# Copies and stores of the last pair of row tiles in a three-way projection

## The chip, the cores and the metric

The kernel runs on one core of a Trainium2 chip. The metric is the device time of one execution in microseconds. A profiled execution gives a span, from the first to the last instruction of the program, and a trace of every engine; the time of that execution is a little longer than its span, because something lies around the program.

The engines in the text: TensorE (PE) multiplies matrices into accumulator banks; VectorE (DVE) and ScalarE (ACT) copy and add; GpSimd (POOL) prepares sums of the input; SyncE (SP) issues most of the transfers; ACT issues some. The transfers themselves run on 16 DMA engines that SP's and ACT's queues share.

## What is computed

```python
def reference(x, w_qkv):           # x: 16 x 512 x 768, w_qkv: 768 x 2304, float32
    qkv = np.matmul(x, w_qkv)
    hidden = x.shape[-1]
    q = qkv[..., :hidden]
    k = qkv[..., hidden:2*hidden]
    v = qkv[..., 2*hidden:]
    return np.stack([q, k, v], axis=0).astype(np.float32)
```

So 8192 rows of 768 numbers are multiplied with one matrix of 768 x 2304, and the 2304 result columns go to three outputs of 768 columns each.

## The kernel before

**Tiles.** Rows are taken in 32 pairs p of two tiles of 128 rows (`NP` = 32). Of the 2304 columns, 2048 are done as two "quads" q of 1024 columns, and 256 columns in between (`REM`) as a plain product, the remainder. A quad of a pair is a block matrix of 2 x 2 blocks, each 128 rows by 512 columns (`CB`): c11, c12 for the first row tile, c21, c22 for the second. It is made with seven block products instead of eight (a Strassen-like scheme): weight sums `ts` are made once, input sums `s` for every pair, and products 1 to 7 of a quad are added up in two accumulator banks x and y and in the output tile.

**Who does what in a quad.** `product(u, n, ps, start)` (line 258 is its matmul) is three matmuls of 128x512. `do(u, n)` issues product n and what takes its result out of the banks:

- n = 1 and 2: product 1 into x, copied to c11 by ACT (L267), product 2 into a third bank, added to c11 by DVE (L280).
- n = 6: on top of x; ACT copies x to c12 (L286).
- n = 5: into y; nothing is taken out.
- n = 7: on top of x; ACT copies x to c22 (L292), then DVE adds y to c22 (L293).
- n = 4: on top of x; ACT copies x to c21 (L296).
- n = 3: on top of y; DVE adds y to c12 (L299).

**Where blocks lie in the outputs.** The first quad has columns 0 to 1023, the second 1280 to 2303, and an output ends every 768 columns. So c12 and c22 of the first quad and c11 and c21 of the second lie across two outputs, 256 columns in each; the other blocks lie in one. Each block is 256 KB.

**Order.** The order on every engine is written out by hand. The pairs before the last go through `two` and `plain`/`summed`; the last `plain` call has `stored` set, and its two quads c and d are stored block by block with `store_cols` on SP's queue. Then `last(a, b)` does pair 31, whose quads are a (q = 0) and b (q = 1): product 1 of both; the remainder of the first row tile; product 2 of both, each with a store of c11; product 6 of both; products 5 and 7 of a with a store of c22, then those of b; products 4 and 3 of a with stores of c21 and c12, then those of b; the remainder of the second row tile. `store_cols(u, r, lo, hi, *engs)` (L404 is its transfer) cuts a block at the border of an output and issues a transfer per piece, each on the next queue of `engs`; all are on SP but for c21 of a, on ACT, and the first half of c21 of b, also on ACT. `rem_stored` multiplies the remainder into one bank (L316), has ACT copy its 256 columns (L414), and issues the store on ACT's queue (L416).

**Semaphores of the transfers.** The recording layer gives the transfers of SP and ACT eight semaphores in turn. A transfer first waits until the one that used its semaphore before has landed, and SP at the end of the program (L690) waits for all eight. Waits between engines are put in by the same layer from the tiles and banks that instructions read and write.

Of the kernel before, what the change touches and what calls it, by code (L numbers as in the profile page):

```python
# [10 lines left out]
def kernel(  # L11
# [20 lines left out]
    nc = tc.nc  # L32
    P = 128
    G = 32
    B, T, H = x.shape
    M = B * T
# [5 lines left out]
    NP = M // (2 * P)  # L42
    CB = 512
    REM = N3 - 4 * CB
    Q_OFF = (0, 2 * CB + REM)
# [4 lines left out]
    ident = mybir.ActivationFunctionType.Identity  # L50
    add = mybir.AluOpType.add
# [3 lines left out]
    out_flat = out.rearrange("s b t h -> s (b t) h")  # L55
# [184 lines left out]
    def quad(p, q, pool=o_pool, tag="o"):  # L240
        u = Quad()
        u.p, u.q = p, q
        u.o = pool.tile([P, 2, 2 * CB], fp32, name="o", tag=tag)
        u.x = u.y = u.z = None
        return u

    def product(u, n, ps, start):
        t1, t2, t3, t4 = ts[u.q]
        if n <= 2:
            h = (n - 1) * KH  # L250
            lhs = [xb[u.p][:, h + j, :P] for j in range(KH)]
            rhs = [b1[u.q][:, h + j, :] for j in range(KH)]
        else:
            k, t = {3: (4, b22[u.q][:]), 4: (0, t4), 5: (1, t1), 6: (2, t2), 7: (3, t3)}[n]
            lhs = [sr[u.p][:, k, j, :] for j in range(KH)]
            rhs = [t[:, j, :] for j in range(KH)]
        for j in range(KH):
            nc.tensor.matmul(  # L258
                ps[:], lhs[j], rhs[j],
                start=(start and j == 0), stop=(j == KH - 1), skip_group_check=True,  # L260
            )

    def bank():
        return ps_pool.tile([P, CB], fp32, name="ps")

    def evacuate(u):
        nc.scalar.activation(u.o[:, 0, :CB], u.x[:], ident)  # L267

    def do(u, n, out=True):
        c11, c12 = u.o[:, 0, :CB], u.o[:, 0, CB:]  # L270
        c21, c22 = u.o[:, 1, :CB], u.o[:, 1, CB:]
        if n == 1:
            u.x = bank()
            product(u, 1, u.x, True)
            if out:
                evacuate(u)
        elif n == 2:
            u.z = bank()
            product(u, 2, u.z, True)
            nc.vector.tensor_tensor(c11, c11, u.z[:], op=add)  # L280
        elif n == 6:
            first = u.x is None
            if first:
                u.x = bank()
            product(u, 6, u.x, first)
            nc.scalar.activation(c12, u.x[:], ident)  # L286
        elif n == 5:
            u.y = bank()
            product(u, 5, u.y, True)
        elif n == 7:  # L290
            product(u, 7, u.x, False)
            nc.scalar.activation(c22, u.x[:], ident)  # L292
            nc.vector.tensor_tensor(c22, c22, u.y[:], op=add)  # L293
        elif n == 4:
            product(u, 4, u.x, False)
            nc.scalar.activation(c21, u.x[:], ident)  # L296
        elif n == 3:
            product(u, 3, u.y, False)
            nc.vector.tensor_tensor(c12, c12, u.y[:], op=add)  # L299
# [14 lines left out]
    def rem_row(p, r, ps):  # L314
        for j in range(KT):
            nc.tensor.matmul(  # L316
                ps, xb[p][:, j, r * P:(r + 1) * P], w_rem[j // KH][:, j % KH, :],
                start=(j == 0), stop=(j == KT - 1), skip_group_check=True,
            )
# [15 lines left out]
    def two(a, b, early, u=None):  # L335

        do(a, 1)
        do(b, 1, u is None)
        if u is None:
            early()  # L340
            rem(a.p)()()
        else:
            middle(u)
            copied = rem(a.p, between=lambda: third(u))
            evacuate(b)
            early()
            copied()()
            fourth(u)
            load_x(a.p + 3, nc.sync)
        do(a, 2)  # L350
        do(b, 2)
        summed(a, b)

    def summed(a, b, between={}, store=True):

        parts = {7: (1, CB, 2 * CB), 4: (1, 0, CB), 3: (0, CB, 2 * CB)}
        for i, (u, n) in enumerate(
            ((a, 6), (b, 6), (a, 5), (a, 7), (b, 5), (b, 7), (a, 4), (a, 3), (b, 4), (b, 3))
        ):
            do(u, n)  # L360
            if store == "parts" and n in parts:
                store_cols(u, *parts[n], nc.sync)
            elif n == 3 and store:
                store_quad(u)
            between.get(i, lambda: None)()
# [14 lines left out]
    def plain(a, b, c, d, early, rem_c, stored=False):  # L380

        add_first(a)
        add_first(b)
        rem(a.p)()()
        do(c, 1)
        do(d, 1)
        early()
        rem_c()
        do(c, 2)
        do(d, 2)  # L390
        add_second(a)
        add_second(b)
        if stored:
            for u in (c, d):
                store_cols(u, 0, 0, CB, nc.sync)

    def store_cols(u, r, lo, hi, *engs):

        c = Q_OFF[u.q] + lo
        end = Q_OFF[u.q] + hi  # L400
        while c < end:
            n = min(end, (c // H + 1) * H)
            row = (2 * u.p + r) * P
            engs[0].dma_start(  # L404
                out_flat[c // H, row:row + P, c % H:c % H + n - c],
                u.o[:, r, c - Q_OFF[u.q]:n - Q_OFF[u.q]],
            )
            c, engs = n, engs[1:] + engs[:1]

    def rem_stored(p, r):  # L410
        ps = bank()
        rem_row(p, r, ps[:, :REM])
        o = or_pool.tile([P, 2, REM], fp32, name="orem")
        nc.scalar.activation(o[:, 0, :], ps[:, :REM], ident)  # L414
        row = (2 * p + r) * P
        nc.scalar.dma_start(out_flat[1, row:row + P, R_OFF - H:R_OFF - H + REM], o[:, 0, :])  # L416

    def last(a, b):

        do(a, 1)  # L420
        do(b, 1)
        rem_stored(a.p, 0)
        for u in (a, b):
            do(u, 2)
            store_cols(u, 0, 0, CB, nc.sync)
        do(a, 6)
        do(b, 6)
        for u in (a, b):
            do(u, 5)
            do(u, 7)  # L430
            store_cols(u, 1, CB, 2 * CB, nc.sync)
        for u in (a, b):
            do(u, 4)
            store_cols(u, 1, 0, CB, *((nc.scalar, ) if u is a else (nc.scalar, nc.sync)))
            do(u, 3)
            store_cols(u, 0, CB, 2 * CB, nc.sync)
        rem_stored(a.p, 1)


# [130 lines left out]
    u = quad(2, 0)  # L570
# [72 lines left out]
    for p in range(ND + 3, NP - 1, 2):  # L643
        first = p == ND + 3
# [13 lines left out]
        a, b = quad(p, 0), quad(p, 1)  # L658
        summed(a, b, {5: turned} if first else {}, False)
        c, d = quad(p + 1, 0), quad(p + 1, 1)  # L660
        final = p + 3 >= NP
        plain(a, b, c, d, early, lambda: rem(c.p)()(), final)
        summed(c, d, {} if final else {0: lambda: transpose(p + 3, 2, 0)}, "parts" if final else True)
    last(quad(NP - 1, 0), quad(NP - 1, 1))


# [28 lines left out]
```

## Time and profile before

| | |
|---|---|
| median of 3 runs | 359.57 us (359.56 to 359.7) |
| profiled execution, its own time | 359.33 us |
| its span | 357.5 us |
| PE busy | 352.0 us, 98% of the span |
| DVE busy | 263.9 us, 74% |
| ACT busy | 185.0 us, 52% |
| POOL busy | 177.3 us, 50% |
| read and written | 32.24 MB and 75.50 MB, 301 GB/s over the span |
| granted TensorE clock | 1.0 |

How to read the lines shown later. In the chain of waits in order of time, a row is the start in us, the length in us, who worked, and how many instructions. In a timeline a row is start, length, engine, source line, operation, output and input tile, shapes and count; in brackets stands the engine's idle time just before and who ended it. `SPq` and `ACTq` are the queues' issuing instructions, which do not make the engine busy. A row of the waits of a queue has who waited for what, the total in us, how often, and the longest. A row of the stretches has the stretch, its length, the busy time and instruction count of PE, weight loads, DVE, ACT and POOL, the granted clock, the share of the 16 DMA engines that was busy (it can come out a little over 1), and GB/s.

### The profile page before, as it was taken

The page shows a single profiled execution, that of the slowest core. Times are in us where ns is not written, and L with a number is a line of the kernel's source. Part 1 is how long each engine was busy: PE and PEld are TensorE (multiplying, and loading weights), DVE is VectorE, ACT ScalarE, POOL GpSimd, SP SyncE. Part 2 cuts the span into 40 slices and gives each one's busy share as a digit, 9 for nine tenths or more (in the row PEclk, how much of TensorE's full clock was granted, in tenths as well). Part 3 has the DMA queues.
Part 4 walks back from the last instruction along what each step waited for, and adds up shares of the span by engine and source line. Part 5 has one row for each costly group of instructions (what it writes and reads, how often), then busy time and mean ns, then how long its engine had stood idle before and what let it go on. Part 6 is the DMA issues. An engine that isn't in the chain of part 4 may idle for free.

```text
span 357.5 us, 5339 instructions
## 1 busy us (share of the span) xinstructions
PE 352.0 (98%) x1776; PEld 252.1 (71%) x1776; DVE 263.9 (74%) x308; ACT 185.0 (52%) x317; POOL 177.3 (50%) x184
## 2 busy tenths in 40 slices
PE   8999999999999999999999999999999999999995
PEld 3474677768677686877768677686877768677674
DVE  3789876796877869777695877869777695877643
ACT  4587755445454653645445454653645455454653
POOL 0031773376466453666535466453666535466420
PEclk9999999999999999999999999999999999999999
DMA  7997999999989998999979899798999979896497
GB/s 296 376 357 236 334 373 340 368 325 342 313 297 340 278 346 206 338 271 307 348 198 386 220 335 312 223 389 215 351 247 329 322 208 386 221 319 247 175 355 265
DMA packets 82203, 108.10 MB, mean 302 GB/s; under 512 B 5120, under 2 KB 62208, under 8 KB 82176
## 3 DMA queue, kind: packets, MB, share of 16 engines
q1 hardware_dynamic: 75072, 102.39, 85.6%
q10 hardware_dynamic: 7104, 5.38, 5.6%
q8 instruction: 14, 0.23, 0.3%
q14 instruction: 13, 0.11, 0.1%
HBM read 32.24 MB, written 75.50 MB: 301 GB/s over the span
## 4 chain that ended last, share of the span: by engine, by line
PE 97%; DMA 2%; ACT 0%; SPq 0%; issue 0%
PE ps L258 79%; PE ps L316 12%; PE ps L486 6%; DMA xin<-in_x_dram 2%; PE ps L185 0%; ACT xc L166 0%; SPq L162 0%; ACT orem L414 0%
## 5 line engine op out<-in xcount | busy, mean ns | idle before, releaser
L258 PE MATMUL ps<-t,s 128*128 128x512 f32 x720 | 177.9, 395 | 0.0
L258 PEld LDWEIGHTS ps<-t,s 128*128 128x128 f32 x720 | 135.0, 188 | 29.6 <-ACT o L267 0.2
L155 DVE STREAM_TRANSPOSE xf<-xin 128x768 f32<-128x768 f32 (+1 forms) x45 | 93.3, 2075 | 2.9 <-DMA xin<-in_x_dram 2.9
L258 PE MATMUL ps<-b,xb 128*128 128x512 bf16 x360 | 85.4, 380 | 0.0
L293 DVE TENSOR_TENSOR o<-o,ps 128x512 f32<-128x512 f32 x58 | 39.9, 687 | 55.2 <-ACT o L292 55.2
L205 POOL CAST xb<-xf 128x1536 bf16<-128x1536 f32 x28 | 41.1, 1466 | 57.0 <-DVE xf L155 57.0
L225 POOL TENSOR_TENSOR s<-xf 128x384 fp32r<-128x384 f32 x29 | 31.0, 1067 | 72.7 <-DVE xf L155 71.0
L258 PEld LDWEIGHTS <-xb 128*128 128x128 bf16 x360 | 33.9, 98 | 36.8 <-issue 4.2
L292 ACT ACTIVATE o<-ps 128x512 f32<-128x512 f32 x58 | 34.7, 598 | 43.6 <-PE ps L258 43.6
L299 DVE TENSOR_TENSOR o<-o,ps 128x512 f32<-128x512 f32 x60 | 41.1, 687 | 20.0 <-PE ps L258 18.8
L258 PE MATMUL ps<-b,s 128*128 128x512 f32 x180 | 50.6, 389 | 0.0
L296 ACT ACTIVATE o<-ps 128x512 f32<-128x512 f32 x60 | 35.9, 598 | 24.6 <-PE ps L258 22.1
L373 DVE TENSOR_TENSOR o<-o,ps 128x512 f32<-128x512 f32 x78 | 47.8, 681 | 0.0
L316 PE MATMUL ps<-w_rem,xb 128*128 128x256 bf16 x384 | 47.3, 273 | 0.0
L286 ACT ACTIVATE o<-ps 128x512 f32<-128x512 f32 x60 | 35.9, 599 | 19.2 <-PE ps L258 15.5
L316 PEld LDWEIGHTS <-xb 128*128 128x128 bf16 x384 | 37.4, 98 | 11.4 <-issue 0.5
L330 ACT ACTIVATE orem<-ps 128x512 f32<-128x512 f32 x31 | 18.5, 597 | 49.5 <-PE ps L316 35.2
L258 PEld LDWEIGHTS ps<-b,s 128*128 128x128 f32 x180 | 33.8, 188 | 7.1
L226 POOL TENSOR_TENSOR s<-s,xf 128x384 fp32r<-128x384 f32 x29 | 29.5, 1019 | 2.3
L227 POOL TENSOR_TENSOR s<-xf 128x384 fp32r<-128x384 f32 x29 | 29.5, 1016 | 0.0
L229 POOL TENSOR_TENSOR s<-xf,s 128x384 fp32r<-128x384 f32 x29 | 29.3, 1009 | 0.0
L377 ACT ACTIVATE o<-ps 128x512 f32<-128x512 f32 x26 | 15.5, 598 | 16.8 <-PE ps L258 16.1
(46 smaller groups left out, 158.6 us busy)
## 6 DMA issues: line engine op xcount, KB each, us to landing
out_dram<-o SPq DMA_DIRECT2D x60, 768.0 KB, 4.6
out_dram<-o SPq DMA_DIRECT2D x67, 256.0 KB, 3.7
xin<-in_x_dram SPq DMA_DIRECT2D x88, 192.0 KB, 5.7
out_dram<-orem SPq DMA_DIRECT2D x31, 256.0 KB, 2.3
xin<-in_x_dram ACTq DMA_DIRECT2D x24, 192.0 KB, 4.5
st<-in_w_qkv_dram SPq DMA_DIRECT2D x5, 768.0 KB, 8.0
out_dram<-o SPq DMA_DIRECT2D x15, 128.0 KB, 2.7
xin<-in_x_dram SPq DMA_DIRECT2D x2, 768.0 KB, 4.9
```

What stands on the lines that cost most here:

```text
L155: nc.vector.transpose(turned[:, g:g + n], rows[:, g:g + n])
L205: nc.gpsimd.tensor_copy(out=xb[p][:], in_=xf[p][:])
L225: 1: lambda g: g.tensor_tensor(s[:, 1], a21, a22, op=add),
L226: 2: lambda g: g.tensor_tensor(s[:, 2], s[:, 1], a11, op=sub),
L258: nc.tensor.matmul(ps[:], lhs[j], rhs[j], start=(start and j == 0), stop=(j == KH - 1), skip_group_check=True,)
L286: nc.scalar.activation(c12, u.x[:], ident)
L292: nc.scalar.activation(c22, u.x[:], ident)
L293: nc.vector.tensor_tensor(c22, c22, u.y[:], op=add)
L296: nc.scalar.activation(c21, u.x[:], ident)
L299: nc.vector.tensor_tensor(c12, c12, u.y[:], op=add)
L316: nc.tensor.matmul(ps, xb[p][:, j, r * P:(r + 1) * P], w_rem[j // KH][:, j % KH, :], start=(j == 0), stop=(j == KT - 1), skip_group_check= ...
L373: dve.tensor_tensor(c, c, u.z[:], op=add)
```

## The change

Four things change, all for the last pair but the second, which also touches the stores of the pair before it, through the same function.

1. In the last pair, ACT copies y to c22 after product 5, and DVE adds x to c22 after product 7.
2. `store_cols` issues one transfer per block; where a block lies across two outputs, the transfer has two pieces of 256 columns per row. All of b's c21 goes from SP.
3. `rem_stored`, used for both row tiles of the last pair: ACT copies the first 128 columns of the remainder, DVE the other 128, both from the same bank.
4. The last block, c12 of b, is added by DVE and stored by SP in two halves of 256 columns.

```diff
@@ in do
         elif n == 5:
             u.y = bank()
             product(u, 5, u.y, True)
+            if u.p == NP - 1:
+                nc.scalar.activation(c22, u.y[:], ident)
         elif n == 7:
             product(u, 7, u.x, False)
-            nc.scalar.activation(c22, u.x[:], ident)
-            nc.vector.tensor_tensor(c22, c22, u.y[:], op=add)
+            if u.p == NP - 1:
+                nc.vector.tensor_tensor(c22, c22, u.x[:], op=add)
+            else:
+                nc.scalar.activation(c22, u.x[:], ident)
+                nc.vector.tensor_tensor(c22, c22, u.y[:], op=add)
@@ store_cols
-    def store_cols(u, r, lo, hi, *engs):
+    def store_cols(u, r, lo, hi, eng):
         c = Q_OFF[u.q] + lo
-        end = Q_OFF[u.q] + hi
-        while c < end:
-            n = min(end, (c // H + 1) * H)
-            row = (2 * u.p + r) * P
-            engs[0].dma_start(
-                out_flat[c // H, row:row + P, c % H:c % H + n - c],
-                u.o[:, r, c - Q_OFF[u.q]:n - Q_OFF[u.q]],
-            )
-            c, engs = n, engs[1:] + engs[:1]
+        n = hi - lo
+        row = (2 * u.p + r) * P
+        src = u.o[:, r, lo:hi]
+        left = (c // H + 1) * H - c
+        if left >= n:
+            dst = out_flat[c // H, row:row + P, c % H:c % H + n]
+        else:
+            assert 2 * left == n
+            first = out_flat[c // H, row:row + P, c % H:H]
+            dst = bass.AP(first.tensor, first.offset, [[H, P], [M * H - H + left, 2], [1, left]])
+            src = src.rearrange("m (s n) -> m s n", s=2)
+        eng.dma_start(dst, src)
@@ rem_stored
-        nc.scalar.activation(o[:, 0, :], ps[:, :REM], ident)
+        half = REM // 2
+        nc.scalar.activation(o[:, 0, :half], ps[:, :half], ident)
+        nc.vector.tensor_copy(out=o[:, 0, half:], in_=ps[:, half:REM])
@@ last
         for u in (a, b):
             do(u, 4)
-            store_cols(u, 1, 0, CB, *((nc.scalar, ) if u is a else (nc.scalar, nc.sync)))
-            do(u, 3)
-            store_cols(u, 0, CB, 2 * CB, nc.sync)
+            store_cols(u, 1, 0, CB, nc.scalar if u is a else nc.sync)
+            if u is a:
+                do(u, 3)
+                store_cols(u, 0, CB, 2 * CB, nc.sync)
+        product(b, 3, b.y, False)
+        for lo in range(0, CB, CB // 2):
+            hi = lo + CB // 2
+            c12 = b.o[:, 0, CB + lo:CB + hi]
+            nc.vector.tensor_tensor(c12, c12, b.y[:, lo:hi], op=add)
+            store_cols(b, 0, CB + lo, CB + hi, nc.sync)
         rem_stored(a.p, 1)
```

## The prediction, made before the changed kernel was run

> **What bounds the kernel now.** I read the page's chain of waits first, then its last entries in order of time, then the timeline of the last 9 us by engine, then the waits of SP's queue and DMA by stretches.
>
> ```profile
> span 357.5 us, 5339 instructions
> PE 97%; DMA 2%; ACT 0%; SPq 0%; issue 0%
> ```
> ```profile
> 344.92 8.11 PE ps L258 x36
> 353.02 0.69 PE ps L316 x6
> 353.71 0.02 issue
> 353.73 0.38 ACT orem L414
> ```
>
> TensorE never stops until 353.71 and the change gives it no less work. What can move is what lies behind: 357.5 - 353.7 = 3.8 us of copying, storing and finishing. Vector, scalar and SP rows of the last pair (start us, us):
>
> ```profile
> 348.98 0.60 ACT L292 ACTIVATE o<-ps 128x512 f32<-128x512 f32 x1 [0.76 <-PE ps L258]
> 350.34 0.60 ACT L292 ACTIVATE o<-ps 128x512 f32<-128x512 f32 x1 [0.76 <-PE ps L258]
> 352.38 0.60 ACT L296 ACTIVATE o<-ps 128x512 f32<-128x512 f32 x1 [0.76 <-PE ps L258]
> 353.73 0.38 ACT L414 ACTIVATE orem<-ps 128x256 f32<-128x256 f32 x1 [0.75 <-PE ps L316]
> 354.15 0.34 ACTq L416 DMA_DIRECT2D out_dram<-orem  x1
> ```
> ```profile
> 349.61 0.69 DVE L293 TENSOR_TENSOR o<-o,ps 128x512 f32<-128x512 f32 x1 [2.62 <-ACT o L292]
> 350.97 0.69 DVE L293 TENSOR_TENSOR o<-o,ps 128x512 f32<-128x512 f32 x1 [0.67 <-ACT o L292]
> 353.06 0.69 DVE L299 TENSOR_TENSOR o<-o,ps 128x512 f32<-128x512 f32 x1 [0.67 <-PE ps L258]
> ```
> ```profile
> SPq L404 <- DMA out_dram<-o: 0.7, 1, 0.7
> ```
> ```profile
> 354.52 0.33 SPq L404 DMA_DIRECT2D out_dram<-o  x1
> ```
>
> The last add ends at 353.06 + 0.69 = 353.75, yet its store is issued at 354.52: SP waits 0.7 for a landing. In the built order each store counts on one of eight semaphores and first waits for the store that used it before; here that is the ACT store issued at 351.65, which lands 2.8 later. The last store lands after 2.2 (landing times are from the narrow views of the store lines), at 356.7; the program ends 0.8 later.
>
> That wait alone is not the bound:
>
> ```profile
> 350.50:351.00 0.50, 0.50 (x4) 0.42 (x3) 0.03 (x1) 0.44 (x1) 0.00 (x0) 1.00 0.06 23
> 352.00:352.50 0.50, 0.50 (x4) 0.42 (x3) 0.39 (x1) 0.12 (x1) 0.00 (x0) 1.00 0.11 33
> 352.50:353.50 1.00, 1.00 (x9) 0.61 (x7) 0.44 (x1) 0.48 (x1) 0.00 (x0) 1.00 1.02 397
> 354.50:355.50 1.00, 0.00 (x0) 0.00 (x0) 0.00 (x0) 0.00 (x0) 0.00 (x0) 1.00 1.10 382
> 355.50:356.20 0.70, 0.00 (x0) 0.00 (x0) 0.00 (x0) 0.00 (x0) 0.00 (x0) 1.00 1.06 402
> ```
>
> The last two columns are the DMA engines' share and GB/s. They are full from 352.5 to 356.2 at about 395 GB/s, 0.33 us per 128 KB, and nearly idle in the half microseconds at 350.5 and 352.0. Eleven pieces of 128 KB pass through that last stretch. The end comes sooner only if bytes move into the idle times ahead of it.
>
> **The change, part by part.** No product is removed or reordered, so 353.71 stands.
>
> *Sooner copied bank.* Now c22 is ACT's copy of x (0.60) after product 7, then DVE's add of y (0.69). Changed, ACT copies y after product 5, 0.67 earlier (ACT is idle 0.76 ahead of each L292), and DVE adds x when product 7 ends. The adds end at 348.98 + 0.69 = 349.67 and 350.34 + 0.69 = 351.03 instead of 350.30 and 351.66, so the stores go out 0.6 sooner. Product 4 must now wait for DVE's read of x instead of ACT's: it starts about 350.3 and 351.7, 0.6 behind the adds, so this costs nothing; without that cover it would be at most DVE's 0.69 - 0.60 = 0.1 on TensorE. SP has nothing later in front of these two stores.
>
> *One transfer per block.* Eight blocks of the last two pairs lie across two outputs and go from two issues to one; SP and ACT save an issue of 0.33 to 0.47 each. The bytes stay. In the last stretch the second half of a's c12 no longer starts at 352.80, and b's c21 goes out whole from SP when ACT's copy ends, 352.38 + 0.60 = 352.98; behind it on SP wait only the two halves, due later. ACT loses its 353.01 issue, which hid in its 0.75 of idling. Fewer issues also turn the eight semaphores more slowly: in the built order each of the last stores waits for one that is eight back and landed by 351.4 in the trace of before, so SP's 0.7 goes.
>
> *Last block in two halves.* One add of 0.69 becomes two of 256 columns. DVE's 128x384 and 128x1536 adds take 547 and 1746 ns: 1.04 ns per column and 147 fixed, so 0.41 each (0.35 if the halves only share the 0.69, 0.69 if all were fixed). Halves end at 353.47 and 353.89; stores follow at about 353.51 and 353.94, against 354.52.
>
> *Remainder by two engines.* ACT copies 128 columns: 384 ns at 256 and 598 at 512 make 0.84 per column and 0.17 fixed, so 0.28 (0.20, the 128x1 row, to 0.38). In the built order DVE's copy waits not for TensorE but for ACT's copy of the same bank. So the two run one after the other: no parallel copy. DVE's 128 columns are not in the trace: 0.28 by the line above, 0.15 if almost only fixed, 0.35 by the 128x384 copy from a bank (354 ns); I take 0.28, as it is another copy of few columns. With 0.03 per handover (349.58 to 349.61) the store goes at 353.73 + 0.28 + 0.03 + 0.28 + 0.03 = 354.35, not 354.15: 0.2 lost, bounds 354.14 to 354.53. Nothing is queued behind it. The pair's first remainder has the same order: ACT 344.95 to 345.23, DVE to 345.54, before DVE's next add (345.66); ACT's store waits 0.2 longer and the next ACT work is at 346.94. It costs nothing.
>
> The Trainium skill, "PSUM — Partial Sum Buffer", section Terms, says that two engines on the same bank and quadrant at once are a collision, reads against reads included; no run here shows one. By that rule the remainder's split cannot pay: 354.35, where copies side by side would give 354.04.
>
> *The sum.* With free engines a 128 KB store landed 1.7 to 1.8 after its issue (350.33, 350.71), so I take 1.4 + 0.33 per 128 KB, and each after the one ahead + 0.33 per 128 KB. Issue, landing: b's c22 351.08, 353.15; a's c21 351.65, 353.8; a's c12 352.42, 354.5; b's c21 353.01, 355.2; the halves 353.51, 355.5 and 353.94, 355.8; the remainder 354.35, 356.15 in the queue (356.08 alone). The last landing moves from 356.67 to 356.15: 0.5 us. With the bounds of the remainder's issue and 1.7 to 1.9 to its landing it is 355.85 to 356.43, a gain of 0.25 to 0.8. The profiled run took 359.33: 357.5 of span and 1.8 around it. Less 0.5 it would be 358.8. The median of the runs, 359.57, is 0.24 above that run, so I forecast **359.05**, own range 358.75 to 359.3.
>
> **Rivals.**
> *No gain (359.55).* The last store, now the remainder, needs as long to land as the 128 KB stores issued at 352.42 to 353.36 did, 2.2 to 2.4: 354.35 + 2.3 = 356.65. For it: all four show it. Against: they stood in a queue that is shorter now, and the two at 350.33 and 350.71 took 1.7 to 1.8.
> The Trainium skill, "DMA: Bandwidth & Descriptors", section Anatomy of one DMA, fits 2.0 us and bytes at 436 GB/s for the GpSimd path: 2.3 us for 128 KB, so an estimate of 356.65 and no gain. This trace, on SP's path, shows 1.7 to 1.8 with free engines.
>
> *More gain (358.75).* The copies do run side by side, or are cheap: store at 353.73 + 0.28 + 0.03 = 354.04 or at the lower bound of 354.14, landing 1.75 later at 355.8 to 355.9, with the queue as short: 0.8. Against it stands the built order's wait, and that the queue alone says 356.1.
>
> *Slower (360.25).* One DMA engine falls behind at an instruction fetch. The queue for these shows 14 of 16 KB in 0.3% of 16 x 357.5 us: 1.2 each. One came in the 1.5 us from 343.0; at 350.5 to 351.0 the share of 0.06 is one engine of 16 still catching up. In the changed kernel the others idle about 0.3 and 0.7 before the last stretch, so a lag up to 1.0 is still worked off. If a fetch falls after 351.9, or lags more than 1.5, the end moves: 356.15 + 1.2 = 357.35, +0.7. Against it: TensorE's instructions, more than half of all, are the same in number and time.
>
> *The change does not do what it says*: for the parallel remainder that is my forecast; the other three parts are in the built order as told.
>
> **How the numbers follow.** Forecast 0.62, no gain 0.16, more gain 0.16, slower 0.06. 0.2% is 0.72 us, about what a measurement of this kernel can tell from no change: faster means under 358.85. That takes 0.1 from the forecast's spread (0.06) and two thirds of more gain: 0.17 in all. Slower than 360.29 is most of the slower rival: 0.05. The rest, 0.78, lies within. The range 358.75 to 359.55 takes in the bounds and most of no gain; it leaves out the slower rival and the ends of the others.
>
> **What would show it.** TensorE's last matmul at 353.7 as now; c22's adds ending at 349.7 and 351.0; no wait of SP for a landing before the last store; DVE's remainder copy starting only after ACT's has ended, and its store as the last issue, near 354.35; the DMA engines' last full stretch ending at 355.6 to 355.8 instead of 356.2. It is wrong if the last store lands at 356.6 after such an issue, if the two copies overlap, or if the full stretch starts no sooner than 352.5.

## The result, and the profile after

| | before | changed |
|---|---|---|
| median of 22 runs each | 359.55 us | 358.99 us |
| ratio | | 0.9986, 95% interval 0.998 to 0.9992 |
| profiled execution, its own time | 359.33 us | 359.14 us |
| its span | 357.5 us | 357.3 us |

The kernel became faster by 0.56 us, 0.14% by the ratio. One of the 22 executions before took 737.67 us, twice the others, which leaves the median where it is (359.54 without it). The two profiled executions differ by less, 0.2 us, and the reason is in the last entries of the chain of waits of the changed kernel (start us, length us, who):

```profile
353.29 0.69 PE ps L321 x6
354.00 0.29 ACT orem L423
354.31 0.29 DVE orem L424
```

TensorE ends at 353.98 in this execution, 0.27 later than the 353.71 of before, though it has the same work in the same order. This is scatter of the loading stage: ACT's fourth remainder copy starts at 44.70 before and at 44.96 here, and from it to the last one it is 309.03 and 309.04 us. In the eleven other profiled executions below, that first mark lies anywhere from 44.8 to 45.4 and the stretch behind it is always 309.0. So single executions are compared by their *tail*: the span less the start of ACT's last remainder copy. It is 3.78 us before (357.51 - 353.73) and 3.35 us changed (357.35 - 354.00): 0.43 less. The time from issue to landing of the store that lands last, first before (c12 of b, issued at 354.52), then changed (the remainder, issued at 354.63):

```profile
DMA to landing us min/median/max: 2.2/2.2/2.2
```
```profile
DMA to landing us min/median/max: 1.9/1.9/1.9
```

So the last landing is 2.9 us after ACT's last copy starts before, and 2.5 us changed; the table below has it to 0.01 from the trace.

The page's own chain in share of the span gives GpSimd 15% and VectorE 6% for the changed kernel, but 19 matmul records are missing from this trace (1757 of 1776), so the chain can lose TensorE there. In the repeat of the same kernel, with all 1776, TensorE has 93% of the chain.

The end, by timeline: the last adds and copies of the changed kernel, and the issues of its last two stores.

```profile
349.32 0.69 DVE L295 TENSOR_TENSOR o<-o,ps 128x512 f32<-128x512 f32 x1 [2.11 <-PE ps L258]
350.68 0.69 DVE L295 TENSOR_TENSOR o<-o,ps 128x512 f32<-128x512 f32 x1 [0.67 <-PE ps L258]
353.33 0.75 DVE L452 TENSOR_TENSOR o<-o,ps 128x256 f32<-128x256 f32 x2 [0.67 <-PE ps L258]
354.00 0.28 ACT L423 ACTIVATE orem<-ps 128x128 f32<-128x128 f32 x1 [0.75 <-PE ps L321]
354.31 0.29 DVE L424 COPY orem<-ps 128x128 f32<-128x128 f32 x1 [0.23 <-ACT orem L423]
354.63 0.34 ACTq L426 DMA_DIRECT2D out_dram<-orem  x1
```
```profile
354.29 0.41 SPq L416 DMA_DIRECT2D out_dram<-o  x1
```

Both adds of c22 start as product 7 ends, with no ACT copy in front. The last block's halves take 0.75 together, and DVE's copy of the remainder is released by ACT's. The DMA engines over the same stretches as before (share and GB/s are the last two columns):

```profile
350.50:351.00 0.50, 0.50 (x4) 0.42 (x3) 0.32 (x1) 0.03 (x1) 0.00 (x0) 1.00 0.14 49
352.00:352.50 0.50, 0.50 (x4) 0.42 (x3) 0.50 (x1) 0.00 (x0) 0.00 (x0) 1.00 0.51 201
352.50:353.50 1.00, 1.00 (x8) 0.67 (x7) 0.33 (x2) 0.60 (x1) 0.00 (x0) 1.00 1.04 404
354.50:355.50 1.00, 0.00 (x0) 0.00 (x0) 0.10 (x1) 0.00 (x0) 0.00 (x0) 1.00 1.09 382
355.50:356.20 0.70, 0.00 (x0) 0.00 (x0) 0.00 (x0) 0.00 (x0) 0.00 (x0) 1.00 0.86 297
```

The engines are half busy at 352.0 to 352.5, where before they had a share of 0.11, and run dry before 356.2, where before they were full up to it, although everything else in this execution is 0.27 later.

### The profile page after: what moved, and what is told of

The parts are those of the page before. It is cut to its first block, busy times and chain, and to the rows that moved or that the text cites. A ratio compares the mean times of both kernels' runs of the same rounds, so it can differ in the third digit from the quotient of the medians.

```text
span 357.3 us, 5318 instructions
## 1 busy us (share of the span) xinstructions
PE 351.2 (98%) x1757; PEld 252.5 (71%) x1776; DVE 264.1 (74%) x311; ACT 185.1 (52%) x317; POOL 177.3 (50%) x184
## 4 chain that ended last, share of the span: by engine, by line
PE 74%; POOL 15%; DVE 6%; issue 3%; DMA 2%; ACT 0%; SPq 0%
PE ps L258 56%; PE ps L321 12%; PE ps L503 6%; DVE xf L155 6%; POOL xb L205 5%; POOL s L226 3%; POOL s L225 3%; POOL s L227 3%; DMA xin<-in_x_dram 2%; ACT xc L166 0%; PE ps L185 0%; DVE o L304 0%; SPq L162 0%; DVE orem L424 0%; ACT orem L423 0%
## 5 line engine op out<-in xcount | busy, mean ns | idle before, releaser
L258 PE MATMUL ps<-b,xb 128*128 128x512 bf16 x343 | 81.6, 379 | 1.1
L298 DVE TENSOR_TENSOR o<-o,ps 128x512 f32<-128x512 f32 x56 | 38.5, 688 | 52.5 <-ACT o L297 52.5
L304 DVE TENSOR_TENSOR o<-o,ps 128x512 f32<-128x512 f32 x59 | 40.4, 687 | 19.9 <-PE ps L258 18.7
L378 DVE TENSOR_TENSOR o<-o,ps 128x512 f32<-128x512 f32 x78 | 47.8, 681 | 0.0
```

The costliest lines, as they stand in the source:

```text
L258: nc.tensor.matmul(ps[:], lhs[j], rhs[j], start=(start and j == 0), stop=(j == KH - 1), skip_group_check=True,)
L378: dve.tensor_tensor(c, c, u.z[:], op=add)
```

## The experiments

In the table, "landing" is the last landing of any store, counted from the start of ACT's last remainder copy; the same zero is used for the issue of the last pair's last c12 store (its second half where it is halved) and of the remainder's store. The ratio is to the kernel before, run on the same chip.

| kernel | landing | tail | c12 issue | remainder issue | ratio, 95% interval |
|---|---|---|---|---|---|
| before | 2.94 | 3.78 | 0.78 | 0.41 | |
| whole change | 2.51 | 3.35 | 0.29 | 0.63 | 0.9986, 0.998 to 0.9992 |
| whole change, again | 2.50 | 3.34 | 0.29 | 0.63 | 0.999, 0.9982 to 0.9999 |
| part 1 alone | 2.55 | 3.45 | 0.10 | 0.41 | 0.9992, 0.9983 to 1.0001 |
| part 2 alone | 2.99 | 3.82 | 0.05 | 0.41 | 1.0003, 0.9994 to 1.0012 |
| part 3 alone | 2.99 | 3.82 | 0.78 | 0.63 | 1.0003, 0.9994 to 1.0012 |
| part 4 alone | 3.00 | 3.95 | 1.21 | 0.41 | 1.0006, 0.9997 to 1.0015 |
| all but part 1 | 3.03 | 3.87 | 0.30 | 0.63 | 1.0004, 0.9996 to 1.0013 |
| all but part 3 | 2.51 | 3.35 | 0.29 | 0.41 | 0.9991, 0.9982 to 1.0 |
| part 2, one store left out | 2.41 | 3.31 | 0.04 | 0.41 | one execution |
| whole change, two banks | 2.56 | 3.40 | 0.33 | 0.42 | one execution |
| parts 1, 2, spread order | 2.40 | 3.30 | -0.64 | 0.41 | 0.999, 0.9981 to 0.9999 |
| the same, three blocks halved | 2.89 | 3.97 | 0.02 | 0.41 | 1.0004, 0.9995 to 1.0013 |

Each kernel has one trace but the whole change, which has two: the second lands within 0.01 us of the first. Its time is 359.37 us against 359.69 before on the same chip, 0.32 less, where 0.4 to 0.6 was expected. The intervals of the times, some 0.6 us wide, are wider than the whole effect, so the tails decide between the theories; the medians go the same way as the tails, no more. From the last landing to the end it is 0.84 us in most of these runs, 0.90 to 0.94 in four and 1.08 in the last of the table; what sets this rest is not shown.

> The whole change once more, beside the next three on one chip. Both theories: time 0.4 to 0.6 us less than before; tail (span less the start of ACT's last remainder copy) 3.35 against 3.78.

**Part 1 alone: ACT copies y after product 5, DVE adds x after product 7.**

The new lines of the diff (shortened):

```diff
             product(u, 5, u.y, True)
+            if u.p == NP - 1:
+                nc.scalar.activation(c22, u.y[:], ident)
...
+            if u.p == NP - 1:
+                nc.vector.tensor_tensor(c22, c22, u.x[:], op=add)
```

> The kernel before with part 1 alone (ACT copies y to c22 after product 5, DVE adds x after product 7). Tail = span less the start of ACT's last remainder copy; before 3.78 us, after 3.35. Theory 'bytes into idle time': the two c22 stores leave 0.6 sooner, the last full DMA stretch loses 256 KB or starts 0.5 sooner, and the time falls by 0.4 to 0.55 us, tail 3.25 to 3.4: all of the whole change's gain. Rival 'SP's semaphore wait' (the 0.7 before the last store is the bound): the wait is still there, shorter only as far as ACT's c21 store lands sooner; the gain then follows the last store's issue and not the start of the stretch, 0.3 to 0.6. Rival 'all four parts share': 0.1 to 0.2.

The landing comes 0.39 sooner, 0.9 of what the whole change gains (0.43), so "all four parts share" falls. The DMA engines of this run, where ACT's last copy starts at 354.30:

```profile
352.10:352.50 0.40, 0.40 (x3) 0.35 (x2) 0.23 (x1) 0.09 (x1) 0.00 (x0) 1.00 0.05 15
352.50:353.00 0.50, 0.50 (x4) 0.39 (x3) 0.46 (x1) 0.05 (x1) 0.00 (x0) 1.00 0.93 365
```

The full stretch begins at 352.5, 1.8 before that copy; in the kernel before it begins at the same reading of the clock, but there ACT's last copy starts at 353.73, so it is 1.2 before it. This run does not yet separate the theory of the idle time from that of SP's wait: c21 of a lands 0.70 sooner too, so the last c12 store no longer waits for it and leaves at 0.10. The next run separates them.

At 3.45 the tail is a little longer than the 3.25 to 3.4 expected: the time from the last landing to the end is 0.90 here and 0.84 in the whole change. The time is 359.42 against 359.69, 0.27 less where 0.4 to 0.55 was expected, and its interval takes in no change.

**Part 2 alone: one transfer per block.** The diff is that of `store_cols`, and `nc.scalar if u is a else nc.sync` for c21.

> The kernel before with part 2 alone (one transfer per block, b's c21 whole on SP). SP's wait of 0.7 for a landing before the last store goes, so this store is issued at about 353.8 instead of 354.5 while no byte is ready sooner. Theory 'bytes into idle time': the last full stretch still starts at 352.5 with the same 1.4 MB, so no gain, 0.0 within 0.1, tail 3.7 to 3.8. Rival 'SP's semaphore wait': the last store lands 0.5 to 0.7 sooner and the time falls by as much, tail 3.1 to 3.3.

This is the run that separates the two theories. The last store, c12 of b, is issued right after its add and not 0.7 later (the waits of SP's queue and the issue itself, part 2 alone, its last 4.5 us):

```profile
SPq L693 <- DMA out_dram<-o: 2.1, 4, 0.6
SPq L411 <- DVE o L299: 0.3, 1, 0.3
```
```profile
354.00 0.34 SPq L411 DMA_DIRECT2D out_dram<-o  x1
```

In this stretch no store (L411) waits for a landing any more; L693 is the end of the program. The issue is at 0.05 instead of 0.78, yet the last landing is at 2.99 instead of 2.94. The DMA engines of this run, by stretches:

```profile
352.20:352.70 0.50, 0.50 (x4) 0.42 (x3) 0.42 (x1) 0.09 (x1) 0.00 (x0) 1.00 0.03 6
352.70:353.70 1.00, 1.00 (x9) 0.63 (x7) 0.41 (x1) 0.51 (x1) 0.00 (x0) 1.00 0.96 371
353.70:354.70 1.00, 0.22 (x3) 0.00 (x0) 0.28 (x1) 0.38 (x1) 0.00 (x0) 1.00 1.05 376
354.70:355.70 1.00, 0.00 (x0) 0.00 (x0) 0.00 (x0) 0.00 (x0) 0.00 (x0) 1.00 1.10 394
355.70:356.40 0.70, 0.00 (x0) 0.00 (x0) 0.00 (x0) 0.00 (x0) 0.00 (x0) 0.82 1.04 388
```

They are idle just before 352.7 and full from there to 356.4, as long as before: 3.7 us. The c12 store that left sooner does land 0.29 sooner (2.66 instead of 2.94), but the remainder's store, now behind it, lands 0.69 later (2.99 instead of 2.30). Here an issue moved forward inside a full stretch changes which store is last, and not when the last one lands.

**Part 3 alone: the remainder copied by ACT and DVE.**

```diff
-        nc.scalar.activation(o[:, 0, :], ps[:, :REM], ident)
+        half = REM // 2
+        nc.scalar.activation(o[:, 0, :half], ps[:, :half], ident)
+        nc.vector.tensor_copy(out=o[:, 0, half:], in_=ps[:, half:REM])
```

> The kernel before with part 3 alone (remainder copied half by ACT, half by DVE). Both theories: DVE's copy starts after ACT's has ended, the remainder's store is issued 0.2 us later than with ACT alone (0.62 to 0.65 after the start of ACT's copy, instead of 0.42). Theory 'bytes into idle time': it hides in the full queue, time 0.0 to +0.1. If a remainder store bounds the end: +0.2. If the copies ran side by side: store 0.1 sooner, time 0.0 to -0.1.

The copies of this kernel, by timeline:

```profile
354.20 0.28 ACT L415 ACTIVATE orem<-ps 128x128 f32<-128x128 f32 x1 [0.75 <-PE ps L316]
354.51 0.29 DVE L416 COPY orem<-ps 128x128 f32<-128x128 f32 x1 [0.29 <-ACT orem L415]
354.84 0.34 ACTq L418 DMA_DIRECT2D out_dram<-orem  x1
```

DVE had been idle for 0.29 and waited for ACT. The store leaves 0.22 later than with ACT alone, and the last landing, which is that of c12, moves by 0.05: the delay hides in the queue, as expected.

**Part 4 alone: the last block in two halves.** The diff is that of `last` with the old `store_cols`.

> The kernel before with part 4 alone (last block added and stored in two halves). SP still waits for ACT's c21 store to land before the first half's store (same semaphore in turn), so the halves go at about 354.5 and 354.9. Theory 'bytes into idle time': no gain, -0.05 to +0.15, tail 3.75 to 3.95. If halving the last block as such pays: -0.2 to -0.3, tail 3.5.

The first half's store waits for the same landing as before (0.78), the second follows at 1.21, and the last lands 0.06 later. Halving by itself brings nothing.

**All but part 1.** Part 1's diff undone in the changed kernel.

> The whole change without part 1 (c22 made as before: ACT copies x after product 7, DVE adds y). Theory 'bytes into idle time': nothing is ready sooner before the last stretch, so the gain is lost although the other three parts are in: time 0.0 (within 0.15) of before, tail 3.7 to 3.9. Rival 'all four parts share': 0.2 to 0.4 less than before, tail 3.4 to 3.6.

b's c21 leaves whole at -0.73, its last block's halves at -0.22 and 0.30 instead of 0.78, the remainder 0.22 later than before, and nothing is gained: landing 3.03. With the run of part 1 alone, this shows part 1 both needed and nearly enough.

**All but part 3.**

> The whole change without part 3 (ACT alone copies the remainder). The remainder's store is issued about 0.42 after the start of ACT's copy instead of 0.63. Theory 'the queue ahead of it is full': it lands hardly sooner, 2.4 to 2.5 after that start instead of 2.51, tail 3.25 to 3.35, time 0.0 to 0.1 less than the whole change. Rival 'the serial copy bounds the end': all of its 0.2 comes back, landing at 2.3, tail 3.15.

The remainder's store leaves at 0.41 instead of 0.63 and lands at 2.51 either way. The split costs 0.22 of latency, and the queue in front of it hides all of it.

**Fewer bytes in the last stretch.** Part 2 alone, with one store left out:

```diff
             do(u, 3)
-            store_cols(u, 0, CB, 2 * CB, nc.sync)
+            if u is b:
+                store_cols(u, 0, CB, 2 * CB, nc.sync)
```

> The kernel before with part 2 alone, and the store of a's c12 in the last pair left out: 256 KB fewer among the bytes of the last full DMA stretch, nothing ready sooner. With part 2 alone the last landing was 2.99 us after the start of ACT's last remainder copy. Theory 'the bytes of the last stretch set the end': 256 KB at 0.33 us per 128 KB are 0.67, so the last landing comes at 2.3 to 2.4, tail 3.1 to 3.25. Rival 'latency behind the last issue' (last store issued at 0.41 landing 2.57 later): unchanged, 2.9 to 3.0.

256 KB less, and the last landing is 0.58 sooner (2.99 to 2.41, just outside the 2.3 to 2.4 expected) with the last issue unchanged at 0.41. The rival of a fixed latency behind the last issue falls. It is 0.09 short of the 0.67 that the bytes are worth; probably because the queue is now short enough for the issues to matter, which no run shows. The share falls to 0.99 where before it was 1.05 to 1.10:

```profile
353.80:354.80 1.00, 0.24 (x3) 0.00 (x0) 0.29 (x1) 0.38 (x1) 0.00 (x0) 1.00 0.99 360
354.80:355.80 1.00, 0.00 (x0) 0.00 (x0) 0.00 (x0) 0.00 (x0) 0.00 (x0) 1.00 0.99 368
```

**The remainder in two banks.** `rem_stored` of the changed kernel, with two banks (new lines, the matmul's flags left out):

```diff
+        ends = [bank(), bank()]
         for j in range(KT):
+            for h in range(2):
+                nc.tensor.matmul(ends[h][:, :half], xb[p][:, j, r * P:(r + 1) * P],
+                    w_rem[j // KH][:, j % KH, h * half:(h + 1) * half], ...)
+        nc.scalar.activation(o[:, 0, :half], ends[0][:, :half], ident)
+        nc.vector.tensor_copy(out=o[:, 0, half:], in_=ends[1][:, :half])
```

> The whole change with the remainder's two halves multiplied into two banks (12 matmuls of 128 columns in place of 6 of 256, each with its own weight load), ACT copying from one and DVE from the other. Theory 'the shared bank orders the copies': DVE's copy now starts with ACT's, within 0.1 us, instead of 0.31 after it, and the store is issued 0.3 to 0.4 after the start of ACT's copy instead of 0.63. Rival 'the shared output tile orders them': 0.63 as in the whole change. The 12 weight loads of 98 ns take up to 0.5 us longer than the six, so TensorE ends later and the time as a whole may well be above the whole change's.

```profile
353.61 0.75 DVE L458 TENSOR_TENSOR o<-o,ps 128x256 f32<-128x256 f32 x2 [0.67 <-PE ps L258]
354.24 0.28 ACT L429 ACTIVATE orem<-ps 128x128 f32<-128x128 f32 x1 [0.71 <-PE ps L424]
354.30 0.29 DVE L430 COPY orem<-ps 128x128 f32<-128x128 f32 x1
354.66 0.34 ACTq L432 DMA_DIRECT2D out_dram<-orem  x1
```

DVE's copy starts 0.06 after ACT's instead of 0.31; both still write one output tile. So it is the shared bank that orders the two. In the built order DVE's copy now waits for TensorE and no longer for ACT. Even so the store leaves at 0.42, no earlier than the 0.41 with ACT alone: a copy of 128 columns takes 0.28 or 0.29 where one of 256 takes 0.38, and DVE's copy starts last: the matmuls of the two banks end at 354.25, just after ACT's copy has started on the bank that was complete, and DVE's starts 0.05 behind them. So the store just misses the 0.3 to 0.4 expected. ACT's last copy, the zero of the table, starts 0.04 sooner against the stores in this run, so the last landing is as good as that of the whole change.

**Another order of the products.** Parts 1 and 2, and in `last`:

```diff
+        blocks = {7: (1, CB, 2 * CB), 4: (1, 0, CB), 3: (0, CB, 2 * CB)}
+        for u, n in ((a, 5), (a, 7), (b, 5), (a, 3), (b, 7), (a, 4), (b, 3), (b, 4)):
+            do(u, n)
+            if n in blocks:
+                store_cols(u, *blocks[n], nc.sync)
```

> Parts 1 and 2, without 3 and 4, and the last pair's products in another order: after 6 of both quads come 5, 7 of a, 5 of b, 3 of a, 7 of b, 4 of a, 3 of b, 4 of b, then the remainder; all blocks are stored by SP. Blocks then leave spread out, the ones of a sooner: by 'bytes into idle time' the last stretch has four 256 KB blocks less one and the remainder behind b's c22 (at -2.0 us from ACT's last copy) and lands at about 2.3, tail 3.1 to 3.2, so 0.15 to 0.25 less than the whole change and 0.6 to 0.7 less than before. If product 4 has to wait for DVE's adds, TensorE's end moves by up to 0.1 and eats part of it. Rival 'the end is the latency behind the last matmul': no gain over the whole change without its split remainder.

Landing 2.40, tail 3.30: 0.11 and 0.05 less than the whole change, where 0.15 to 0.25 was expected. I had taken five blocks and the remainder for less work than they are: the dense stretch begins, with a's c12, some 1.75 us before ACT's last copy, as in the whole change with b's c22, and holds the same eleven pieces. Where the 0.11 comes from is not shown. It beats the kernel before (ratio 0.999), but its time, 359.33, cannot be told from the 359.37 of the whole change on the same chip. TensorE's last stretch is 309.0 us in this order too.

**The same, with three blocks halved.** The adds and stores of a's c12, b's c22 and b's c12 in two halves each, as part 4 does it for one.

> The spread order with the adds and stores of a's c12, b's c22 and b's c12 in halves, remainder by ACT alone. Theory 'bytes into idle time': the first halves are stored 0.28 sooner, the dense stretch starts as much sooner, and the last landing is bounded by the latency of the remainder's and b's c21 stores: 2.2 to 2.35 after the start of ACT's last copy (spread order 2.40, whole change 2.51), tail 3.1 to 3.25, time 0.1 to 0.25 under the whole change and 0.5 to 0.7 under before. Rival 'each further issue on SP costs more than it brings': 2.4 or more.

A miss, and the rival was right. The last two issues of SP's queue in this run, b's c12's second half and b's c21:

```profile
353.91 0.41 SPq L416 DMA_DIRECT2D out_dram<-o  x1
354.41 0.41 SPq L416 DMA_DIRECT2D out_dram<-o  x1
```

SP issues one store every 0.50 us, six stores in a row, so b's c21, issued at -0.05 in the unhalved order, leaves at 0.52 and lands at 2.89. In the last microsecond before ACT's last copy the DMA engines have a share of 1.06 in the unhalved order and of 0.75 here: they run dry between the stores.

## Why the prediction was right

The forecast was 359.05 and the median is 358.99; the forecast's mechanism is what the runs show. That the two times lie within 0.06 us is in part luck: 0.5 us of gain were forecast, while the tails, which leave the scatter out, give 0.43, the median here 0.56 and that of the repetition 0.32. By its steps:

- *That wait alone is not the bound.* Shown by part 2 alone and by all but part 1: the wait gone, nothing gained.
- *The end comes sooner only if bytes move into the idle times.* Shown from both sides: part 1, the only part that moves bytes ahead of the full stretch, gives 0.39 of the 0.43 us, and without it nothing is gained; a block left out gives 0.58.
- *Sooner copied bank.* Adds ending 0.63 sooner were forecast. Counted from ACT's last copy, b's c22 leaves at -2.60 instead of -2.04 and a's at -3.96 instead of -3.40, 0.56 sooner: the sum let DVE's add start where ACT's copy had started (4.75 before the last copy), and it starts 0.07 later (354.00 - 349.32 = 4.68). TensorE lost nothing: its last stretch of 309.0 us is unchanged.
- *Last block in two halves.* Forecast 0.41 for each add, one behind the other. Each does take 0.41 to 0.42, but the second starts 0.34 after the first, so the two take 0.75 together and not 0.83. The second half's store left at 0.29 and not 0.21 all the same, because SP had issued the first half's 0.51 before it; the sum had left out this spacing of SP's issues.
- *Remainder by two engines.* Forecast one after the other, 0.28 and 0.28, store 0.62 after ACT starts; measured 0.28, 0.29 and 0.63. The rule of the Trainium skill cited there ("PSUM — Partial Sum Buffer", section Terms: no two engines on one bank and quadrant at once) is what the built program keeps; no run here let them collide, and the run with two banks shows the order gone with the shared bank.
- *The sum.* It came to a last landing of 2.42 after ACT's last copy (356.15 - 353.73); measured 2.51. Store by store the forecast is met within 0.05 up to b's c21 (1.48); the three stores of 128 KB behind it land at 1.82, 2.18 and 2.51, 0.34, 0.36 and 0.33 apart, 1.03 in place of three times 0.33. So the mechanism was right, and the last three stores were 0.04 short; the other 0.05 are small differences and roundings ahead of them.
- *The profiled run would take 358.8.* It took 359.14. The step that failed is "353.71 stands": it stands against the 309 us before it, not against the start, which scatters by some 0.6 us between executions. Medians average this out only in part, as the gains of 0.56 and 0.32 show.

The rivals: *no gain* needed 2.3 us from the remainder's issue to its landing. It took 1.88, with a little queue in front, against 1.7 to 1.8 with free engines; in part 3 alone, where the last block's store had not yet been issued in front of it, 1.72. The fit in the Trainium skill, "DMA: Bandwidth & Descriptors", section Anatomy of one DMA, which is for GpSimd's path, gave an estimate of 2.3 us for 128 KB; this path shows 1.72 and 1.88. *More gain* asked for copies side by side; they are not, and the run without the split shows that it would not have helped, because the queue alone sets 2.51. *Slower*, by an instruction fetch in the last stretch, did not come: the last landing is within 0.09 of the sum, and the twelve other executions show no last landing later than 3.03.

## What to carry to other kernels

At the end of a kernel, look at whether the DMA engines are full before asking what the last store waits for: if they are, as here, fewer bytes or bytes that become ready ahead of the full stretch move the end, and an earlier issue inside it does not. Of four plausible repairs here, one paid, and it was the one furthest from the last instruction. In this program two engines that copy from one bank took turns, so sharing a copy between them made its store 0.22 us later; and where the queue issued a store every half microsecond, cutting three blocks in halves made the queue the bound.

## What was not expected

In the thirteen profiled executions the scatter, about 0.6 us, arises in the first 45 us; the 309.0 us behind them repeat to 0.02 us. That makes single traces, counted from a late mark, sharper than eleven timed runs. And a store that is issued back to back with another costs SP 0.50 us, though its row shows only 0.41 of it.
